# Weight pieces of 512 columns instead of 256 for v and for the last gate of a hybrid decoder layer, and v as a whole ahead of the recurrent branch

## The chip, the cores and the metric

The kernel runs on one core of one Trainium2 chip. What counts is the time of an execution on the device, in microseconds (us); the figure for a kernel is the median of its runs. A profile is of one execution, whose own time stands beside it.

## What is computed

One decoder layer in fp32 on 512 positions of width 1024, and a last RMSNorm:

```python
h = rmsnorm(x, norm_mix_g)
u_x, u_g, q, k, v, g_lru, g_att = split(h @ w_in)           # w_in: 1024 x 7168
c = causal_depthwise_conv(u_x, conv_w, conv_b)
y_lru = rg_lru(c, w_rgate, b_rgate, w_igate, b_igate, lam) * gelu(u_g)
y_att = stick_breaking_attention(q, k, v)                    # 16 heads of 64
merged = sigmoid(g_lru) * (y_lru @ w_br_lru) + sigmoid(g_att) * (y_att @ w_br_att)
x = x + merged @ w_out
x = x + square(relu(rmsnorm(x) @ w_mlp_up)) @ w_mlp_down     # 4096 wide
x = x + sigmoid(rmsnorm(x) @ w_ple_gate) * (p @ w_ple)
out = rmsnorm(x, norm_final_g)
```

The multipliers of a norm are folded: a product is made with x times the gain, and the reciprocal root of a row is multiplied in afterwards, where the rows lie on partitions.

## The kernel before

**Products.** Every fp32 product is made of three matmuls. `split` (L51 to L53) cuts a tile into a rounded part `hi` (a cast on ScalarE, L52) and the rest `lo` (a subtraction on VectorE, L53); `prod` (L115 to L121) then adds hi·hi (L119), hi·lo (L120) and lo·hi (L121) in one accumulator. For most products the weights are the stationary operand and 512 positions of the activations stream by (`proj`, L125). v and the last gate are the other way round, since their rows (positions) must lie on partitions: 128 positions of the activations are stationary and the weight columns stream by, 256 at a time. Such a product is named by its block of positions `tb` (0 to 3) and its piece of columns.

**Weights.** `load_raw` (L46) fetches 512 KB into one of three buffers `raw`, `split` writes it to `whi` and `wlo`, also three buffers each. `next_half` (L103) hands out the piece that is ready and starts on the next of the list `halves`; so loads run two or three pieces ahead of the matmuls, and a cast waits until the matmuls are done with the buffer that it overwrites.

**Order.** Engines work off their instructions in order. The order in the program is set by a scheduler that places instructions by modelled times; the code sets dependences, buffers and a few priorities.

**v before** (L214 to L273, L382 to L386). x arrives in eight row tiles of 128 x 512, and with each the rows of the first weight piece. `xg` is x times the gain, split. v is made in four pieces of 256 columns: `v0` row tile by row tile as x comes in, `v1` and `v2` behind it, all with xg; `v_evac` multiplies them by `rcol`, the reciprocal roots, on the way out. Meanwhile the sums of squares are made, turned into `rcol`, spread over all partitions by matmuls (`bc_x`, L186), and `hT`, the normed x, is made from them (L262, then L52 and L53). All later projections take hT. `v3` follows only behind the recurrent branch, with hT. Accumulators: a pool `pst` of four banks for v0 and v2, `pp` of three banks for v1 and for all that `proj` makes up to the attention, so that the first product of the recurrent branch, `ps_ux`, takes a bank of `pp`.

**Recurrent branch** (L276 to L380). Eight products `ps_ux`, each followed by a convolution on VectorE and the small gate products `pg`; then eight products `ps_ug`. The second half of the recurrence, `lru_mid(1)`, is a chain of 128 x 2048 instructions on ScalarE and VectorE, with four scans (L347) and the multiplication L379 at its end. Attention tiles (`qs`, `kh`) lie where the branch's tiles lay, so their first writer waits for L379.

**Last gate** (L589 to L654). For four pieces of 256 columns and four blocks of positions, `gate_rows` makes a product `pgt`; `gate_post` applies the sigmoid (L609), multiplies by `ple` and adds to x (L610, L611), sums squares (L612) and multiplies by the last gain (L614). `last_norm` scales and stores a block.

Of the kernel before, what the change touches and what calls it, by code (L numbers as in the profile page):

```python
# [31 lines left out]
def hybrid_layer(ctx, tc, xT, pT, vecs, gfin, gates, w_in, w_bl, w_ba, w_out,  # L32
# [185 lines left out]
    def v_evac(ch, tb, ps, scale):  # L218
        hi = vs[:, 2 * ch:2 * ch + 2, tb, 0:4:3, :]
        lo = vs[:, 2 * ch:2 * ch + 2, tb, 1:3, :]  # L220
        src = ps.rearrange("p (a b d) -> p a b d", a=2, b=2)
        if scale is None:
            split(hi, lo, src)
        else:
            sc.activation(hi, src, AF.Copy, scale=scale)
            for a in range(2):
                ve.scalar_tensor_tensor(lo[:, a], src[:, a], scale, f32(hi[:, a]),
                                        op0=ALU.mult, op1=ALU.subtract)

    def v_pairs(act, w, tb):  # L230
# [368 lines left out]
    def gate_rows(tb, q):  # L599
        t = slice(tb * P, (tb + 1) * P)  # L600
        ps = pq.tile([P, 256], F32, tag="pp", name=f"pgt{tb}_{q}")
        prod(ps, [(h3[:, 0, k, t], h3[:, 1, k, t], wq[q][k // 4][0][:, k % 4, :],
                   wq[q][k // 4][1][:, k % 4, :]) for k in range(KT)])
        return ps

    def gate_post(tb, q, ps):
        c = slice(q * 256, (q + 1) * 256)
        sg = sgs[(q + tb) % 4]
# [25 lines left out]
    wq.append([next_half("pg1_0")])  # L634
    behind = ctx.enter_context(ExitStack())
    behind.enter_context(tc.issue_after(scaled.ins))
    for i, (hi, lo) in ((3, (wb3[:, 0], wb3[:, 1])), *((4 + j, (wb1[:, 2 * j], wb1[:, 2 * j + 1]))
                                                       for j in range(4))):
        split(hi, lo, load_raw(w_pg[i // 2][:, (i % 2) * 1024:(i % 2 + 1) * 1024], f"pg{i}"))
        if i % 2 == 0:  # L640
            wq.append([])
        wq[i // 2].append(tuple(t.rearrange("p (k n) -> p k n", k=4) for t in (hi, lo)))
# [84 lines left out]
```

## Time and profile before

| | us |
|---|---|
| median of three runs | 945.73 |
| the three runs | 943.81, 945.73, 948.19 |
| the profiled execution, its own time | 946.11 |
| its span, from the first instruction to the last | 944.0 |
| TensorE busy in the span | 929.5 |
| VectorE busy | 542.4 |
| ScalarE busy | 471.3 |

The profile page gives busy times, a chain of work that ended last, and groups of instructions; the trace answers for single lines, tiles and stretches of time. TensorE's time is listed as PE, its weight loads as PEld, VectorE as DVE, ScalarE as ACT. A matmul's duration in the listing is from its start to its modelled end and overlaps the next one's; the pace is the distance from start to start.

### The profile page before, as it was taken

To read this page: it belongs to the slowest core of one execution; us is meant where nothing else is said; L and a number is where in the kernel's file an instruction comes from. 1 tells how busy PE (TensorE), PEld (TensorE's weight loads), DVE (VectorE), ACT (ScalarE), POOL (GpSimd) and SP (SyncE) were. 2 spreads that over 40 slices of the span, in tenths; PEclk is the share of its full clock that TensorE was granted. 3 is DMA by queue.
4 is the path that set the end of the run, shared out by engine and by line. 5 is a ranking of instruction groups with operands and counts; after the bars stand their busy time and mean duration, and the time that the engine had idled before them with its cause. 6 is when DMAs were issued, how large, how long until landed. Compare 5 with 4: busy or idle time off the path is not lost.

```text
span 944.0 us, 12123 instructions
## 1 busy us (share of the span) xinstructions
PE 929.5 (98%) x4634; PEld 790.9 (84%) x4634; DVE 542.4 (57%) x818; ACT 471.3 (50%) x751; POOL 67.9 (7%) x147
## 2 busy tenths in 40 slices
PE   8999999999999999999999999999999999999996
PEld 7988888888888888888888888888888888888896
DVE  6796947688998986534655433333333333344476
ACT  6567676667776765412334444541214554333443
POOL 0010000133233332000000000000000000000000
PEclk9999999999999999999999999999999999999998
DMA  6241222211222222432232223323223223222312
GB/s 220 95 134 67 90 90 85 95 68 67 68 68 68 67 68 68 173 111 95 90 109 92 90 90 104 119 90 101 100 90 108 94 89 107 94 90 90 112 45 90
DMA packets 25401, 89.42 MB, mean 95 GB/s; under 512 B 2944, under 2 KB 3200, under 8 KB 25088
## 3 DMA queue, kind: packets, MB, share of 16 engines
q1 hardware_dynamic: 24768, 87.61, 27.5%
q10 hardware_dynamic: 576, 1.05, 0.3%
q8 instruction: 36, 0.59, 0.3%
q14 instruction: 21, 0.17, 0.1%
HBM read 86.55 MB, written 2.10 MB: 94 GB/s over the span
## 4 chain that ended last, share of the span: by engine, by line
PE 95%; ACT 2%; DVE 1%; DMA 1%; issue 1%; SPq 0%; ACTq 0%
PE ps_up L119 6%; PE dn L121 6%; PE ps_up L121 6%; PE dn L119 6%; PE dn L120 6%; PE ps_up L120 6%; PE t L445 2%; PE pgt L120 2%; PE pgt L121 2%; PE pgt L119 2%; PE ps_gl L121 2%; PE ps_k L121 2%; PE ps_q L119 2%; PE ps_ga L121 2%; PE ps_q L120 2%; PE ps_k L119 2%
## 5 line engine op out<-in xcount | busy, mean ns | idle before, releaser
L119 PE MATMUL dn<-ah,whi_dn 128*128 128x512 f32 x256 | 100.2, 391 | 0.0
L119 PE MATMUL ps_up<-h,whi_up 128*128 128x512 f32 x256 | 99.9, 390 | 0.0
L121 PE MATMUL ps_up<-h,wlo_up 128*128 128x512 f32 x256 | 99.7, 390 | 0.0
L121 PE MATMUL dn<-ah,wlo_dn 128*128 128x512 f32 x256 | 99.7, 389 | 0.0
L120 PE MATMUL ps_up<-h,whi_up 128*128 128x512 f32 x256 | 99.6, 389 | 0.0
L120 PE MATMUL dn<-al,whi_dn 128*128 128x512 f32 x256 | 99.6, 389 | 0.0
L52 ACT CAST whi_dn<-raw_dn 128x1024 fp32r<-128x1024 f32 x32 | 33.6, 1053 | 108.3 <-PE dn L120 82.9
L53 DVE TENSOR_TENSOR wlo_up<-raw_up,whi_up 128x1024 fp32r<-128x1024 f32 x32 | 39.2, 1224 | 73.4 <-ACT whi_up L52 73.4
L52 ACT CAST whi_up<-raw_up 128x1024 fp32r<-128x1024 f32 x32 | 33.7, 1054 | 91.3 <-PE ps_up L120 62.9
L53 DVE TENSOR_TENSOR wlo_dn<-raw_dn,whi_dn 128x1024 fp32r<-128x1024 f32 x32 | 39.0, 1222 | 67.6 <-ACT whi_dn L52 67.6
L432 DVE TENSOR_TENSOR_SCAN pr<-r,zero 128x128 f32<-128x128 f32 (+1 forms) x64 | 54.1, 845 | 10.7 <-POOL r L155 10.2
L121 PEld LDWEIGHTS dn<-ah,wlo_dn 128*128 128x128 f32 x256 | 48.1, 188 | 10.1
L121 PEld LDWEIGHTS ps_up<-h,wlo_up 128*128 128x128 f32 x256 | 48.1, 188 | 10.0
L120 PEld LDWEIGHTS ps_up<-h,whi_up 128*128 128x128 f32 x256 | 48.1, 188 | 10.0
L120 PEld LDWEIGHTS dn<-al,whi_dn 128*128 128x128 f32 x256 | 48.1, 188 | 9.8
L119 PEld LDWEIGHTS ps_up<-h,whi_up 128*128 128x128 f32 x256 | 48.1, 188 | 9.8
L119 PEld LDWEIGHTS dn<-ah,whi_dn 128*128 128x128 f32 x256 | 48.1, 188 | 9.7
L155 POOL TENSOR_SCALAR_AFFINE_SELECT r<-r 128x128 f32<-128x128 f32 x64 | 29.8, 466 | 192.6 <-ACT r L428 190.2
L428 ACT ACTIVATE r<-z 128x128 f32<-128x128 f32 (+1 forms) x64 | 28.5, 445 | 27.7 <-PE z L424 27.0
L580 DVE TENSOR_TENSOR d<-dn,sumsq 128x512 f32<-128x512 f32 x16 | 11.1, 692 | 52.1 <-PE dn L121 52.1
L155 POOL TENSOR_SCALAR_AFFINE_SELECT s<-s 128x128 f32<-128x128 f32 x64 | 33.6, 525 | 5.1 <-ACT s L430 3.3
L434 DVE TENSOR_TENSOR s<-s,pr 128x127 f32<-128x127 f32 (+1 forms) x64 | 31.8, 498 | 3.6
(282 smaller groups left out, 2424.0 us busy)
## 6 DMA issues: line engine op xcount, KB each, us to landing
raw_up<-in_w_up_dram SPq DMA_DIRECT2D x32, 512.0 KB, 3.4
raw_dn<-in_w_dn_dram SPq DMA_DIRECT2D x32, 512.0 KB, 3.5
raw_u<-in_w_in_dram SPq DMA_DIRECT2D x16, 512.0 KB, 3.6
raw_qk<-in_w_in_dram SPq DMA_DIRECT2D x16, 512.0 KB, 3.5
raw_gl<-in_w_in_dram SPq DMA_DIRECT2D x8, 512.0 KB, 3.4
raw_ga<-in_w_in_dram SPq DMA_DIRECT2D x8, 512.0 KB, 3.4
raw_bl<-in_w_bl_dram SPq DMA_DIRECT2D x8, 512.0 KB, 3.4
raw_ba<-in_w_ba_dram SPq DMA_DIRECT2D x8, 512.0 KB, 3.4
```

The lines of the kernel that those rows point to most:

```text
L52: sc.copy(hi, src)
L53: ve.tensor_tensor(lo, src, f32(hi), op=ALU.subtract)
L119: pe.matmul(ps, lh, rh, start=(first and i == 0), stop=False)
L120: pe.matmul(ps, lh, rl, start=False, stop=False)
L121: pe.matmul(ps, ll, rh, start=False, stop=(last and i == n - 1))
L155: gp.affine_select(block, block, pattern=[[-1, P]], compare_op=ALU.is_gt, fill=fill, base=0, channel_multiplier=1)
L428: sc.activation(r[:, 0:w], z[:, 0:w], AF.Sigmoid, scale=-0.125)
L432: ve.tensor_tensor_scan(pr[:, 0:w][:, ::-1], r[:, 0:w][:, ::-1], zero.broadcast_to([P, w]), 1.0, op0=ALU.mult, op1=ALU.add)
L434: ve.tensor_tensor(s[:, 0:w - 1], s[:, 0:w - 1], pr[:, 1:w], op=ALU.mult)
L445: turned[kbs[0]] = pe.transpose(pt[:, o:o + P], att[qb][:, kb * P:(kb + 1) * P], ident)
L580: ve.tensor_tensor(t, ps, rs2, op=ALU.mult)
```

## The change

v is made in two pieces of 512 columns, both ahead of the recurrent branch and both with xg. Its weights come in chunks of two row tiles by 512 columns (512 KB as before), eight chunks `v0_0` to `v1_3`. Of the first piece, six row tiles are loaded beside x, in three chunks, and the fourth chunk through `next_half`. The second piece runs chunk by chunk, over the four blocks of positions in each; three of its accumulators are in `pp`, the fourth in `pst`. `v_evac` takes 512 columns: one ScalarE instruction and four on VectorE. The stage `v3` behind the recurrent branch is gone.

The gate has two pieces of 512 columns. For the first, all four blocks run over row tiles 0 to 5, and then over 6 and 7; the second piece of the last block is still made as two of 256. `gate_post` takes 512 columns; the sum of a block's squares has two terms instead of four (three for the last block). The weights are laid out accordingly on the host. The core of the diff:

```diff
-    for i in range(3):
-        order(f"v{i}", w_in[i], 4)
+    for i in range(2):
+        for j in range(4):
+            halves.append((f"v{i}_{j}", w_in[2 * i + j // 2][:, (j % 2) * 1024:(j % 2 + 1) * 1024], 2))
     for i in range(8):
         order(f"u{i}", w_in[4 + i], 8)
-    order("v3", w_in[3], 4)
...
-    for a, b in ((0, 1), (1, 2), (2, 4), (4, 6), (6, 8)):
+    for a, b in ((0, 1), (1, 2), (2, 4), (4, 6)):
+        if a != 1:
+            raw0.append(wp.tile([P, 1024], F32, tag="raw", name=f"raw_v0_{a // 2}"))
         sy.dma_start(x32[:, a:b, :], xT[:, a:b, :])
-        sy.dma_start(raw0[a // 4][:, a % 4:(b - 1) % 4 + 1, :], src0[:, a:b, :])
+        c = slice((a % 2) * 512, ((b - 1) % 2 + 1) * 512)
+        sy.dma_start(raw0[-1][:, c], halves[a // 2][1][:, c])
+    sy.dma_start(x32[:, 6:8, :], xT[:, 6:8, :])
...
-        ps0 = [pst.tile([P, 256], F32, tag="pv", name=f"pv0_{tb}") for tb in range(NB)]
+        ps0 = [pst.tile([P, S], F32, tag="pv", name=f"pv0_{tb}") for tb in range(NB)]
         for k in range(KT):
+            if k == 6:
+                w.append(next_half("v0_3"))
             for tb in range(NB):
-                prod(ps0[tb], v_pairs(xg, w, tb)[k:k + 1], first=(k == 0), last=(k == KT - 1))
+                prod(ps0[tb], v_pairs(xg, w, [k], tb), first=(k == 0), last=(k == KT - 1))
...
-        w = next_pair("v1")
-        psv = [pp.tile([P, 2, 256], F32, tag="pp", name=f"pv1_{i}") for i in range(2)]
-        for tb in range(NB):
-            prod(psv[tb // 2][:, tb % 2, :], v_pairs(xg, w, tb))
...
+        ps1 = [(pp if tb < 3 else pst).tile([P, S], F32, tag="pp" if tb < 3 else "pv", name=f"pv1_{tb}")
+               for tb in range(NB)]
         for tb in range(NB):
             v_evac(0, tb, ps0[tb], rcol[:, tb:tb + 1])
+        for j in range(4):
+            w = [None] * j + [next_half(f"v1_{j}")]
+            for tb in range(NB):
+                prod(ps1[tb], v_pairs(xg, w, [2 * j, 2 * j + 1], tb), first=(j == 0), last=(j == 3))
         for tb in range(NB):
-            v_evac(1, tb, psv[tb // 2][:, tb % 2, :], rcol[:, tb:tb + 1])
-        w = next_pair("v2")
-        for tb in range(NB):
-            ps = pst.tile([P, 256], F32, tag="pv", name=f"pv2_{tb}")
-            prod(ps, v_pairs(xg, w, tb))
-            v_evac(2, tb, ps, rcol[:, tb:tb + 1])
+            v_evac(1, tb, ps1[tb], rcol[:, tb:tb + 1])
...
-        w = next_pair("v3")
-        for tb in range(NB):
-            ps = pp.tile([P, 256], F32, tag="pp", name=f"pv3_{tb}")
-            prod(ps, v_pairs(hT, w, tb))
-            v_evac(3, tb, ps, None)
...
-    wq = [next_pair("pg0")]
-    first = [gate_rows(tb, 0) for tb in range(3)]
+    wq = [[next_half(f"pg0_{j}") for j in range(3)], []]
+    rows = [pq.tile([P, S], F32, tag="pp", name=f"pgt{tb}_0") for tb in range(NB)]
+    for tb in range(NB):
+        gate_rows(rows[tb], tb, range(0, 6))
...
     for tb in range(NB):
-        gate_post(tb, 2, gate_rows(tb, 2))
+        gate_rows(rows[tb], tb, range(6, 8))
+        gate_post(tb, 0, 512, rows[tb])
+    for tb in range(NB):
+        w = 512 if tb < NB - 1 else 256
...
+        for a in range(512, 1024, w):
+            ps = pq.tile([P, w], F32, tag="pp", name=f"pgt{tb}_{a}")
+            gate_rows(ps, tb, range(0, KT), slice(a - 512, a - 512 + w), 1)
```

VectorE before, between the spreading of the norm and the first product of the recurrent branch; `bc_x` is the spread norm, `vs` the evacuated v, `pv2_0` its third piece for the first block:

```order
L262 SCALAR_TENSOR_TENSOR x32_68<-x32_68,vt_67,bc_x_409 128x512 x7
L227 SCALAR_TENSOR_TENSOR vs_105<-pv1_1_293,rcol_279,vs_105 128x128 [waits Activation_49]
L227 SCALAR_TENSOR_TENSOR vs_105<-pv1_1_293,rcol_279,vs_105 128x128
L53 TENSOR_TENSOR hT_106<-x32_68,hT_106 128x512 [waits Activation_49]
L227 SCALAR_TENSOR_TENSOR vs_105<-pv2_0_482,rcol_279,vs_105 128x128 [waits Activation_49]
L227 SCALAR_TENSOR_TENSOR vs_105<-pv2_0_482,rcol_279,vs_105 128x128
L53 TENSOR_TENSOR hT_106<-x32_68,hT_106 128x512 [waits Activation_49] x2
L227 SCALAR_TENSOR_TENSOR vs_105<-pv2_1_510,rcol_279,vs_105 128x128 [waits Activation_49]
L227 SCALAR_TENSOR_TENSOR vs_105<-pv2_1_510,rcol_279,vs_105 128x128
L53 TENSOR_TENSOR hT_106<-x32_68,hT_106 128x512 [waits Activation_49] x4
```

The same place of the changed kernel; `pv1_0` is the second piece of 512 columns for the first block:

```order
L265 SCALAR_TENSOR_TENSOR x32_68<-x32_68,vt_67,bc_x_303 128x512 [waits PE_49]
L265 SCALAR_TENSOR_TENSOR x32_68<-x32_68,vt_67,bc_x_303 128x512 x7
L53 TENSOR_TENSOR wlo_u0_0_457<-raw_u0_0_454,whi_u0_0_456 128x1024 [waits DMAHW7_49,Activation_49]
L53 TENSOR_TENSOR hT_106<-x32_68,hT_106 128x512 [waits Activation_49] x7
L53 TENSOR_TENSOR wlo_u0_1_562<-raw_u0_1_559,whi_u0_1_561 128x1024 [waits DMAHW1_49,Activation_49]
L53 TENSOR_TENSOR hT_106<-x32_68,hT_106 128x512 [waits Activation_49]
L227 SCALAR_TENSOR_TENSOR vs_105<-pv1_0_340,rcol_283,vs_105 128x128 [waits Activation_49]
L227 SCALAR_TENSOR_TENSOR vs_105<-pv1_0_340,rcol_283,vs_105 128x128 x3
```

The evacuations of v's last pieces stood between the parts of hT before, and stand behind all of them now.

TensorE in the changed kernel, at the end of v and the beginning of the recurrent branch; `dg_x3` belongs to the last part of the spreading:

```order
L188 MATMUL bc_x_303<-dg_x3_313,onesf_87 128x128 [waits DVE_49]
L121 MATMUL pv1_3_343<-whi_v1_1_366,xg_113 128x512
L119 MATMUL pv1_0_340<-whi_v1_2_396,xg_113 128x512 [waits Activation_49]
...
L119 MATMUL pv1_0_340<-whi_v1_3_426,xg_113 128x512 [waits Activation_49]
...
L121 MATMUL pv1_3_343<-whi_v1_3_426,xg_113 128x512
L119 MATMUL ps_ux0_558<-hT_106,whi_u0_0_456 128x512 [waits DVE_49,Activation_49]
```

Between the spreading and `ps_ux0` 49 matmuls of v are left, and `ps_ux0` waits for VectorE with its first matmul.

VectorE before, at the end of the recurrent branch; L347 are the scans, L379 the multiplication that ends the branch, `qs0` and `kl` the first tiles of the attention:

```order
L347 SCALAR_TENSOR_TENSOR i1_877<-a1_1347,r1_876 128x512 x3
L53 TENSOR_TENSOR vs_105<-pv3_0_1381,vs_105 128x2x128 [waits Activation_49]
L53 TENSOR_TENSOR vs_105<-pv3_1_1408,vs_105 128x2x128 [waits Activation_49]
L379 TENSOR_TENSOR y_lru_1075<-i1_877,y_lru_1075 128x2048 [waits DVE_49]
L53 TENSOR_TENSOR vs_105<-pv3_2_1435,vs_105 128x2x128 [waits Activation_49]
L53 TENSOR_TENSOR wlo_qk0_1_1518<-raw_qk0_1_1515,whi_qk0_1_1517 128x1024 [waits DMAHW3_49,Activation_49]
L53 TENSOR_TENSOR vs_105<-pv3_3_1462,vs_105 128x2x128 [waits Activation_49]
```

The same place of the changed kernel (the scans are L351, the multiplication L383):

```order
L349 TENSOR_TENSOR r1_786<-r1_786,i1_787 128x2048 [waits Activation_49]
L53 TENSOR_TENSOR wlo_qk1_0_1339<-raw_qk1_0_1336,whi_qk1_0_1338 128x1024 [waits DMAHW2_49,PE_49,Activation_49]
L351 SCALAR_TENSOR_TENSOR i1_787<-a1_1257,r1_786 128x512 [waits DVE_49]
L351 SCALAR_TENSOR_TENSOR i1_787<-a1_1257,r1_786 128x512 x3
L53 TENSOR_TENSOR wlo_qk1_1_1531<-raw_qk1_1_1528,whi_qk1_1_1530 128x1024 [waits DMAHW3_49,PE_49,Activation_49]
L383 TENSOR_TENSOR y_lru_985<-i1_787,y_lru_985 128x2048 [waits DVE_49]
L53 TENSOR_TENSOR wlo_gl0_0_1562<-raw_gl0_0_1559,whi_gl0_0_1561 128x1024 [waits DMAHW4_49,PE_49,Activation_49]
L408 TENSOR_TENSOR qs0_1366<-ps_q0_1304,qs0_1366 64x512 [waits Activation_49]
L411 TENSOR_TENSOR kl_1301<-ps_k0_1335,kh0_1367 64x512 [waits Activation_49]
```

The four evacuations of v3 are gone, and the weights of q and k of the second pair (`qk1`) stand ahead of the scans and of the multiplication. On TensorE three projections (q0, k0, q1, 72 matmuls) follow the last `ps_ug` directly, then the first scores, which read `qs0`, `kh0` and `kl`; before, v3's 96 matmuls came first, and the scores stood behind q0, k0, q1 and four matmuls of k1.

## Rows read from the trace of the kernel before

**Rows 1.** Page: busy time of each engine, its share of the span, instructions.

```profile
PE 929.5 (98%) x4634; PEld 790.9 (84%) x4634; DVE 542.4 (57%) x818; ACT 471.3 (50%) x751; POOL 67.9 (7%) x147
```

**Rows 2.** Waits of TensorE: total us, times, longest us.

```profile
PE pv L119 <- ACT whi_v L52: 2.9, 2, 2.5
...
PE pv L119 <- DVE vs L53: 1.6, 1, 1.6
```

**Rows 3.** Matmul groups of 256 columns (line, shapes, count | busy us, mean ns | idle).

```profile
L119 PE MATMUL pv<-whi_v,xg 128*128 128x256 f32 x96 | 24.3, 301 | 2.9 <-ACT whi_v L52 2.9
L119 PE MATMUL pgt<-wb,h 128*128 128x256 f32 x80 | 22.6, 283 | 0.0
...
L119 PE MATMUL pgt<-whi_pg,h 128*128 128x256 f32 x48 | 13.7, 286 | 0.0
...
L119 PE MATMUL pv<-whi_v,hT 128*128 128x256 f32 x32 | 9.0, 286 | 1.6 <-DVE vs L53 1.6
```

**Rows 4.** Timeline (start us, us, what), TensorE, in the MLP's second half.

```profile
880.41 0.39 PE L121 MATMUL dn<-ah,wlo_dn 128*128 128x512 f32 x1
...
887.21 0.39 PE L121 MATMUL dn<-ah,wlo_dn 128*128 128x512 f32 x1
```

**Rows 5.** Timeline, ScalarE, last gate: the last weight cast, sigmoids of 256 columns.

```profile
904.46 1.05 ACT L52 CAST wb<-raw_pg 128x1024 fp32r<-128x1024 f32 x1 [0.73 <-DMA raw_pg<-in_w_pg_dram]
...
912.42 0.47 ACT L609 ACTIVATE work<-pgt,rs 128x256 f32<-128x256 f32 x1 [0.33 <-PE pgt L121]
...
921.06 0.47 ACT L609 ACTIVATE work<-pgt,rs 128x256 f32<-128x256 f32 x1 [0.89 <-PE pgt L121]
```

**Rows 6.** Timeline, TensorE, the beginning.

```profile
5.84 1.22 PE L119 MATMUL pv<-whi_v,xg 128*128 128x256 f32 x4 [0.43 <-ACT whi_v L52]
...
9.18 0.28 PE L121 MATMUL pv<-whi_v,xg 128*128 128x256 f32 x1
11.94 0.74 PE L119 MATMUL pv<-whi_v,xg 128*128 128x256 f32 x4 [2.48 <-ACT whi_v L52]
```

**Rows 7.** Timeline, ScalarE, the third and fourth row tile of x.

```profile
9.73 1.33 ACT L56 ACTIVATE xg<-x,vt 128x512 fp32r<-128x512 f32 x2 [2.14 <-DMA x<-in_xT_dram]
```

**Rows 8.** Stretches: busy us (count) of PE, PEld, DVE, ACT, POOL; PEclk; DMA; GB/s.

```profile
6.00:8.00 2.00, 2.00 (x14) 2.00 (x15) 1.80 (x4) 1.34 (x3) 0.00 (x0) 1.00 0.76 200
...
12.00:14.00 2.00, 1.78 (x12) 1.58 (x13) 2.00 (x5) 2.00 (x5) 0.00 (x0) 0.94 0.90 363
14.00:16.00 2.00, 2.00 (x12) 2.00 (x11) 2.00 (x5) 2.00 (x5) 0.00 (x0) 0.50 0.79 277
16.00:18.00 2.00, 2.00 (x14) 2.00 (x14) 2.00 (x4) 2.00 (x5) 0.00 (x0) 0.70 0.03 12
```

**Rows 9.** Timeline, VectorE, ahead of the recurrent branch.

```profile
36.51 1.12 DVE L227 SCALAR_TENSOR_TENSOR vs<-pv,rcol,vs 128x128 fp32r<-128x128 f32 x4
...
38.67 5.35 DVE L262 SCALAR_TENSOR_TENSOR x<-x,vt,bc_x 128x512 f32<-128x512 f32 x8
...
47.31 2.48 DVE L53 TENSOR_TENSOR hT<-x,hT 128x512 fp32r<-128x512 f32 x4
...
50.83 1.21 DVE L53 TENSOR_TENSOR wlo_u<-raw_u,whi_u 128x1024 fp32r<-128x1024 f32 x1
```

**Rows 10.** Timeline, TensorE, from the last `ps_ug` through v3.

```profile
145.92 0.39 PE L121 MATMUL ps_ug<-hT,wlo_u 128*128 128x512 f32 x1
...
154.66 0.28 PE L121 MATMUL pv<-whi_v,hT 128*128 128x256 f32 x1
156.50 0.39 PE L119 MATMUL pv<-whi_v,hT 128*128 128x256 f32 x1 [1.56 <-DVE vs L53]
```

**Rows 11.** Timeline, VectorE, from the branch's end to the first kl.

```profile
156.69 2.28 DVE L379 TENSOR_TENSOR y_lru<-i,y_lru 128x2048 f32<-128x2048 f32 x1
...
172.75 0.68 DVE L414 TENSOR_TENSOR kl<-ps_k,kh 64x512 fp32r<-64x512 f32 x1
```

**Rows 12.** Timeline, ScalarE, ahead of the first qs.

```profile
164.92 1.05 ACT L52 CAST whi_qk<-raw_qk 128x1024 fp32r<-128x1024 f32 x1 [3.92 <-PE ps_q L120]
```

More of the change, by code (lines that the diff above doesn't have):

```diff
@@ L99, in hybrid_layer @@
             order(f"dn{h}_{i}", w_dn[8 * h + i], 8)
-    order("pg0", w_pg[0], 4)
-    halves.append(("pg1_0", w_pg[1][:, 0:1024], 4))
+    for j in range(3):
+        halves.append((f"pg0_{j}", w_pg[0][:, j * 1024:(j + 1) * 1024], 2))
     state = {"i": 0, "ready": None}
@@ L218, in v_evac, with v_pairs @@
     def v_evac(ch, tb, ps, scale):
[L219 to L230, printed above, removed]
+        hi = vs[:, 4 * ch:4 * ch + 4, tb, 0:4:3, :]
+        lo = vs[:, 4 * ch:4 * ch + 4, tb, 1:3, :]
+        src = ps.rearrange("p (a b d) -> p a b d", a=4, b=2)
+        sc.activation(hi, src, AF.Copy, scale=scale)
+        for a in range(4):
+            ve.scalar_tensor_tensor(lo[:, a], src[:, a], scale, f32(hi[:, a]),
+                                    op0=ALU.mult, op1=ALU.subtract)
+    def v_pairs(act, w, ks, tb):
         t = slice(tb * P, (tb + 1) * P)
-        return [(act[:, 0, k, t], act[:, 1, k, t], w[k // 4][0][:, k % 4, :], w[k // 4][1][:, k % 4, :])
-                for k in range(KT)]
+        return [(act[:, 0, k, t], act[:, 1, k, t], w[k // 2][0][:, k % 2, :], w[k // 2][1][:, k % 2, :])
+                for k in ks]
     with tc.tile_pool(name="st", bufs=1) as st, \
@@ L589, in hybrid_layer @@
     work = big2.tile([P, 8192], F32, tag="B3", name="work")
-    gf, junk = work[:, 0:1024], work[:, 1024:1280]
+    gf, junk = work[:, 0:1024], work[:, 1024:1536]
     outs = [work[:, 2048 + i * 1024:3072 + i * 1024] for i in range(4)]
-    sgs = [work[:, 6144 + i * 256:6400 + i * 256] for i in range(4)]
+    sgs = [work[:, 6144 + i * 512:6656 + i * 512] for i in range(2)]
     sy.dma_start(gf, gfin.broadcast_to([P, D]))
@@ L597, in hybrid_layer, with gate_rows, gate_post @@
     ssc = const.tile([P, 4 * NB], F32, name="ssc")
-    def gate_rows(tb, q):
+    def gate_rows(ps, tb, ks, c=slice(0, 512), h=0):
         t = slice(tb * P, (tb + 1) * P)
[L601 to L608, printed above, removed]
+        prod(ps, [(h3[:, 0, k, t], h3[:, 1, k, t], wq[h][k // 2][0][:, k % 2, c],
+                   wq[h][k // 2][1][:, k % 2, c]) for k in ks], first=(ks[0] == 0), last=(ks[-1] == KT - 1))
+    def gate_post(tb, a, n, ps):
+        c = slice(a, a + n)
+        sg = sgs[tb % 2][:, 0:n]
         sc.activation(sg, ps, AF.Sigmoid, scale=rs3[:, tb:tb + 1])
@@ L633, in hybrid_layer @@
     wb3 = big.tile([P, 2, 1024], F32R, tag="F1", name="wb3")
-    wq.append([next_half("pg1_0")])
     behind = ctx.enter_context(ExitStack())
@@ L638, in hybrid_layer @@
                                                        for j in range(4))):
[L639 to L642, printed above, removed]
+        split(hi, lo, load_raw(w_pg[i // 4][:, (i % 4) * 1024:(i % 4 + 1) * 1024], f"pg{i}"))
+        wq[i // 4].append(tuple(t.rearrange("p (k n) -> p k n", k=2) for t in (hi, lo)))
     behind.close()
-    for q in range(2):
-        for tb in range(NB):
-            gate_post(tb, q, first[tb] if q == 0 and tb < 3 else gate_rows(tb, q))
     for tb in range(NB):
-        gate_post(tb, 2, gate_rows(tb, 2))
+        gate_rows(rows[tb], tb, range(6, 8))
+        gate_post(tb, 0, 512, rows[tb])
+    for tb in range(NB):
+        w = 512 if tb < NB - 1 else 256
         s012 = fin.tile([P, 1], F32, tag="ss", name=f"ssf{tb}")
-        ve.tensor_reduce(s012, ssc[:, 4 * tb:4 * tb + 3], axis=mybir.AxisListType.X, op=ALU.add)
-        ve.tensor_scalar(s012, s012, 1.0 / D, EPS, op0=ALU.mult, op1=ALU.add)
-        gate_post(tb, 3, gate_rows(tb, 3))
+        for a in range(512, 1024, w):
+            ps = pq.tile([P, w], F32, tag="pp", name=f"pgt{tb}_{a}")
+            gate_rows(ps, tb, range(0, KT), slice(a - 512, a - 512 + w), 1)
+            if a + w == 1024:
+                head = ssc[:, 4 * tb + 1:4 * tb + 2]
+                if w == 256:
+                    ve.tensor_tensor(s012, head, ssc[:, 4 * tb + 2:4 * tb + 3], op=ALU.add)
+                    head = s012
+                ve.tensor_scalar(s012, head, 1.0 / D, EPS, op0=ALU.mult, op1=ALU.add)
+            gate_post(tb, a, w, ps)
         last_norm(tb, s012)
@@ L686, in _layout @@
     wi = wi.reshape(56, P, KT, P)[order].reshape(28, 2, P, KT, P)
-    wi = np.concatenate([wi[:4].transpose(0, 2, 3, 1, 4).reshape(4, P, 2048),
+    wv = wi[:4].reshape(2, 4, P, KT, P).transpose(0, 2, 3, 1, 4).reshape(2, P, 2, 2048)
+    wi = np.concatenate([wv.transpose(0, 2, 1, 3).reshape(4, P, 2048),
                          wi[4:].transpose(0, 2, 1, 3, 4).reshape(24, P, 2048)])
```

29 lines of the change are left out of this document (16 added, 13 removed).

## The prediction

> **What bounds the kernel now.** I read the busy times first: TensorE works 929.5 of 944.0 us, 98% of the span, VectorE 57%, ScalarE 50% [rows 1]. So the change is worth what it does to the pace of TensorE's matmuls and to TensorE's few waits. The list of those waits comes second. Two belong to v: 2.5 us at the start, where the third row tile of x and its weights aren't there yet, and 1.6 us at v3 [rows 2]. Third, the groups of 256 columns: the three lines of a product count alike, so v has 3 × (96 + 32) = 384 such matmuls and the gate 3 × (80 + 48) = 384, and the gate's never waited [rows 3]. Last, the pace, from start to start in undisturbed stretches: 30 matmuls of 512 columns in 887.21 − 880.41 = 6.80 us, 0.2267 us each [rows 4]; three blocks of 24 matmuls of 256 columns between two sigmoids, 921.06 − 912.42 = 8.64 us for 72, 0.1200 us each [rows 5].
>
> **Matmuls: −4.8 us.** All 384 of v and 336 of the gate become 512 wide (the last block's second piece, 48, stays): 360 pairs. A pair takes 2 × 0.1200 = 0.2400 us, one of 512 columns 0.2267: 13.3 ns less, 360 times, 4.8 us (2.6 in v, 2.2 in the gate). TensorE has no cover, so it counts in full. No row shows a matmul of 512 columns with positions stationary. From below the saving is nothing (time by the column); from above it is the 13.3 ns, since the three matmuls of a product in rows 4 have the same form of 128 x 512. I take 13.3, the row of equal shape.
>
> Here a rule speaks against the change. The Trainium skill, "TensorE: Matmul & The Clock Gate", section "Back-to-back issue gap", gives the gap of lone warm matmuls as columns over 2.4 GHz plus 2.5 ns, so that a pair would save only 2.5 ns; 360 pairs would save 0.9 us by it, an estimate. The rows here disagree: they show 120.0 and 226.7 ns, where it has 109 and 216.
>
> **Start: −1.1 us.** Before, TensorE runs two row tiles from 5.84 to 9.30 and sits idle until 11.94, 2.48 us of it listed as waiting for ScalarE's cast [rows 6], which was held by x arriving for 9.73 and by ScalarE's two scaled copies of 1.33 us [rows 7]. The 24 matmuls took 3.46 us instead of 24 × 0.12 = 2.88: 0.6 us of slow beginning. After, each row tile brings 256 KB of weights instead of 128. The first cast is twice as long, +0.2 us (an estimate, counted below); then 24 × 0.2267 + 0.6 = 6.0 us of work, until 12.1. The x tiles three and four arrive behind 0.26 MB more: at the 363 GB/s of the stretch 12 to 14 [rows 8] 0.7 us, so ScalarE begins at 10.4 and TensorE 2.2 us after that as before, plus 0.8 (two wider casts at 0.2, and 0.13 MB more ahead of the third tile's weights, 0.4), at 13.5: a wait of 1.4 us instead of 2.5. Best is 0.6, without the 0.8. With 200 GB/s, the rate of 6 to 8 [rows 8], the 0.52 MB more up to the fourth tile's weights are 2.6 us, TensorE goes on at some 14.7 and the wait is 2.6. I take 1.4, since both tiles are fetched in the busier stretch. Behind that wait stands all of v, as before. Later row tiles have 12 × 0.2267 = 2.7 us of work each, for 512 KB that at 363 GB/s take 1.4: no wait.
>
> **First matmul later: +0.2 us**, the wider cast.
>
> **v3's wait goes: −1.7 us.** TensorE's last matmul before it began at 154.66, the next at 156.50 [rows 10]; less 0.12 that is 1.7. With the stage gone nothing waits there. What is next late is the attention's start, below.
>
> **New wait at `ps_ux0`: +2.4 us.** The second piece's accumulator `pv1_0` has the bank of `pp` that `ps_ux0` takes, so its first matmul waits until VectorE has evacuated `pv1_0`, and in the order that stands behind all of the normed x. From the spreading on, VectorE needs 5.35 for the eight multiplications, 1.21 for weights, 8 × 0.62 for hT, 1.21 for weights and 1.12 for four subtractions [rows 9]: 13.85 us, some 13.4 with the overlaps that the rows show (eight of 0.69 in 5.35). TensorE has 49 × 0.2267 = 11.1 us of v left. The wait is 2.3 to 2.75; I take 2.4. Before, the pieces were evacuated between parts of hT and TensorE ran through. Behind the waiting matmul on TensorE is the whole recurrent branch; ScalarE's copies and VectorE's convolution wait for that, with no work of their own that would hide it. The three other evacuations, 3.4 us, come while `ps_ux0` runs (24 × 0.2267 = 5.4 us) and cost nothing. Scaled evacuations are as many as before, and those of v3 fall away.
>
> **Clock: 0.** After the idle stretch before 11.94 the granted clock fell from 1.00 to 0.50 and then read 0.70 [rows 8], its two levels being 2.4 and 1.2 GHz: 0.06 × 2 + 0.50 × 2 + 0.30 × 2 = 1.7 us of work lost. The wait of 1.6 at v3 isn't the length that was followed by this; 2.48 was. So I expect no fall behind the start's 1.4 (−1.7) and one behind the 2.4 at `ps_ux0` (+1.7). Bounds: −1.7 if neither, +1.7 if both.
>
> **Branch to attention: 0.** Count from T, the end of the last `ps_ug`, 145.92 + 0.23 = 146.15 [rows 10]. v3 covered this place with 96 matmuls. Now TensorE is ready for the first scores after 72 matmuls of q0, k0 and q1, at T + 16.3, and they need `qs0` and `kl`, whose tiles are free only when L379 has ended. That was at 156.69 + 2.28 = 158.97, T + 12.8 [rows 11]. In the new order one weight subtraction of 1.21 replaces 0.73 of v3's ahead of it: T + 13.3. Then come weights 1.21, `qs0` 0.68 and `kl` 0.68: T + 15.9, 0.4 ahead of need. From above: the first `kl` ended at 172.75 + 0.68, T + 27.3 [rows 11], which would be a wait of 11.0. But ScalarE stood 3.92 us for q0's matmuls there [rows 12], which v3 had put back, so I take 0.
>
> **Last gate: 0.** The weights of its second piece are needed after 96 × 0.2267 = 21.8 us instead of 192 × 0.12 = 23.0, and are asked for some 1.4 us later, since the norm's sums, which release them, stand behind 35 matmuls of 512 columns where 54 of 256 stood (7.9 against 6.5 us). The last were cast from 904.46 on [rows 5], for 1.05, and subtracted in 1.21: done at 906.7, now at 908.1. The sigmoid of 912.42 [rows 5] is that of the eighth block, with which the first half of the gate's columns ends, so the need was at about 912.1 and is now at 910.8; for the last weights it is 18 matmuls, 4.1 us, later. Cost 0, at worst the 2.6 by which need and request draw together. The work behind the last matmul is as before.
>
> **Sum.** −4.8 − 1.1 + 0.2 − 1.7 + 2.4 + 0 = −5.0. From the profiled execution's own 946.11 (span 944.0) that is 941.1; it lies 0.4 above the median of 945.73, from which the forecast is 940.7.
>
> **Rivals.**
> - *The clock stays up behind `ps_ux0`.* TensorE's wait there is near the v3 one, which was no cause of a fall; −1.7: 939.0. Against it: 2.4 is nearer to 2.48 than to 1.6.
> - *The start gains nothing.* At 200 GB/s the wait is 2.6 (+1.2) and the clock falls there too (+1.7): 943.6. For it: the first row tiles came at that rate. Against: later ones didn't.
> - *The change doesn't do what it says*, time goes by the column: +4.8, 945.5. The Trainium skill's gap, cited above, would give 944.6, an estimate. For it: no row of this kind; against it: the two paces of rows 4 and 5, both steady.
> - *Slower: the scores wait for the recurrent branch.* If `qs0` and `kl` come late because ScalarE's and VectorE's weight work stands ahead of L379 and of `kl`, TensorE waits up to 11.0 us at T + 16.3: 951.7. From 5.0 us of wait on the kernel is slower than before, from 9.7 on by over 0.5%. For it: the margin is 0.4 us and v3's 13.3 us of cover are gone. Against: of the 27.3 us most was waiting for TensorE itself.
>
> **How the numbers follow.** Chances: forecast 0.46 (940.7, its own range 939.7 to 942.0 from the bounds at the start and at `ps_ux0`), clock up 0.20, start without gain 0.18, columns 0.07, scores 0.09. The range goes from 937.8 (clock up, and the start's best) to 944.9, which leaves out the upper half of the columns' case and most of the scores'. A measurement of this kernel tells some 0.5% from no change, 4.7 us: faster means below 941.0. That takes somewhat over half of the forecast's 0.46 and the 0.20 of the clock: 0.45. Slower is above 950.5, half of the scores' 0.09 and a rest: 0.06. The remaining 0.49 is the same.
>
> **What would show it.** In the changed kernel's groups v and gate read 128x512, and 24 of them in a row take 5.44 us (5.76 if time goes by the column). TensorE's waits list about 1.4 us at the start, none for v's last stage, and one of `ps_ux0` for VectorE's `vs` of about 2.4; the granted clock is 1.00 in the stretches after the start and falls for some 3 us after `ps_ux0` begins. The first scores wait for no `kl` and no `qs`. Wrong would be a wait of several us at the first scores, or at the gate's second piece for its weights, or a start that waits longer than 2.5.

## The result and the profile after

| | before | after |
|---|---|---|
| median, us | 945.73 | 941.22 |
| the runs, us | 943.81 to 948.19 (7) | 940.31 to 942.0 (7) |
| the profiled execution, its own time | 946.11 | 941.22 |
| its span | 944.0 | 939.5 |

The ratio of after to before is 0.9948, with a 95% interval from 0.9934 to 0.9962: 4.5 us less, where the forecast was 940.7, 5.0 less.

The page of the changed kernel, busy times, which answer [rows 1]:

```profile
PE 925.9 (99%) x4274; PEld 772.0 (82%) x4274; DVE 542.5 (58%) x795; ACT 466.5 (50%) x719; POOL 67.4 (7%) x147
```

TensorE is busy 3.6 us less and has 360 matmuls fewer. Its waits (total us, times, longest us), which answer [rows 2]:

```profile
PE ps_ux L119 <- DVE vs L227: 2.5, 1, 2.5
PE wt L164 <- POOL onesf L151: 1.2, 1, 1.2
PE pv L119 <- ACT whi_v L52: 0.8, 1, 0.8
```

v3's wait and that of the third row tile are gone; the new one at `ps_ux0` is 2.5 long. The 0.8 stands ahead of the first matmul of v. The groups (line, shapes, count | busy us, mean ns | idle), which answer [rows 3]:

```profile
L120 PE MATMUL pv<-wlo_v,xg 128*128 128x512 f32 x64 | 25.6, 400 | 0.1
...
L120 PE MATMUL pgt<-wb,h 128*128 128x512 f32 x32 | 12.4, 389 | 0.0
L120 PE MATMUL pgt<-wlo_pg,h 128*128 128x512 f32 x24 | 9.4, 390 | 0.0
```

The beginning on TensorE (start us, us, what), which answers [rows 6]:

```profile
6.20 2.07 PE L119 MATMUL pv<-whi_v,xg 128*128 128x512 f32 x4 [0.79 <-ACT whi_v L52]
8.07 0.63 PE L120 MATMUL pv<-wlo_v,xg 128*128 128x512 f32 x1
8.50 0.63 PE L121 MATMUL pv<-whi_v,xg 128*128 128x512 f32 x1
...
10.62 1.07 PE L119 MATMUL pv<-whi_v,xg 128*128 128x512 f32 x4
...
13.34 1.11 PE L119 MATMUL pv<-whi_v,xg 128*128 128x512 f32 x4
```

The first row tile takes 10.62 − 6.20 = 4.42 us, the second 13.34 − 10.62 = 2.72, which is 12 × 0.2267. The third begins without a wait and takes 16.48 − 13.34 = 3.14. From `ps_ux0` to the first scores and in the gate, on TensorE, which answers [rows 10]:

```profile
56.43 0.47 PE L119 MATMUL ps_ux<-hT,whi_u 128*128 128x512 f32 x1 [2.54 <-DVE vs L227]
...
156.47 0.39 PE L121 MATMUL ps_ug<-hT,wlo_u 128*128 128x512 f32 x1
156.69 0.39 PE L119 MATMUL ps_q<-hT,whi_qk 128*128 128x512 f32 x1
...
173.01 0.39 PE L420 MATMUL z<-kh,qs 128*128 128x128 f32 x2
173.24 0.39 PE L421 MATMUL z<-kl,qs 128*128 128x128 f32 x2
...
885.00 0.48 PE L119 MATMUL pgt<-whi_pg,h 128*128 128x512 f32 x1
...
930.27 0.28 PE L121 MATMUL pgt<-wb,h 128*128 128x256 f32 x1
```

In the kernel before the same places stand at 47.44 (`ps_ux0`), 145.92 (last `ps_ug`), 159.48 (first q0), 887.79 and 935.14 (first and last of the gate). From these starts the 4.5 us of the two spans can be booked, beside the forecast's terms. v's matmuls are booked at the paces of the prediction, which both traces of the changed kernel show again in v (12 matmuls in 2.72 us). "Start" is what is left of `ps_ux0`'s start without v's matmuls and without its own wait: 47.44 − 288 × 0.1200 = 12.88 before, 56.43 − 2.54 − 192 × 0.2267 = 10.36 after.

| us | forecast | the two traces |
|---|---|---|
| v's matmuls (192 × 13.3 ns) | −2.6 | −2.6 |
| start, with its clock | −1.1 + 0.2 − 1.7 | −2.5 |
| wait at `ps_ux0` | +2.4 | +2.5 |
| clock behind `ps_ux0` | +1.7 | +1.6 (100.04 to the last `ps_ug`, 98.48 before) |
| v3's wait | −1.7 | −1.8 (13.56 from the last `ps_ug` to q0, now 0.22; less 96 × 0.12) |
| q0 to the gate | 0 | 0 (728.31 both) |
| gate | −2.2 | −2.1 (47.35, now 45.27) |
| behind the last matmul | 0 | +0.4 (8.9, now 9.2) |
| sum | −5.0 | −4.5, as the spans |

### The profile page after: what moved, and what is told of

Read it like the earlier page. It is cut to its first block, busy times and chain, and to the rows that moved or that the text cites. A ratio compares the mean times of both kernels' runs of the same rounds, so it can differ in the third digit from the quotient of the medians.

```text
span 939.5 us, 11336 instructions
## 1 busy us (share of the span) xinstructions
PE 925.9 (99%) x4274; PEld 772.0 (82%) x4274; DVE 542.5 (58%) x795; ACT 466.5 (50%) x719; POOL 67.4 (7%) x147
```

## The experiments

**The change once more.** The same kernel, in the rounds of the next three.

> The changed kernel once more, on the chip and in the rounds in which its parts are timed. By the result so far: 4.5 us less than before (ratio 0.995). Its profile, from another execution, tells which of the stretches are steady: the matmul pace of v, 0.2267 us, the wait of about 2.5 us at ps_ux0 with a lower clock behind it, and no wait at the attention's start should stand again; where in the first 10 us the clock rises may differ.

941.45 us, ratio 0.9953 (0.9940 to 0.9967). The profiled execution, of 939.84, shows the wait of 2.55 at `ps_ux0` and no lower clock behind it. Stretches of this execution (TensorE's busy time and count stand first behind the length, the granted clock stands third from the end):

```profile
54.00:56.00 2.00, 0.06 (x1) 0.00 (x0) 2.00 (x5) 1.62 (x2) 1.82 (x2) 1.00 0.15 27
56.00:58.00 2.00, 1.40 (x6) 1.21 (x7) 2.00 (x9) 1.95 (x2) 1.81 (x3) 1.00 0.60 240
58.00:60.00 2.00, 2.00 (x11) 1.62 (x10) 2.00 (x10) 1.43 (x2) 0.00 (x0) 1.00 0.00 0
60.00:62.00 2.00, 2.00 (x11) 1.65 (x10) 1.97 (x3) 0.00 (x0) 0.00 (x0) 1.00 0.11 18
```

The same in the first trace of the changed kernel:

```profile
54.00:56.00 2.00, 0.00 (x0) 0.00 (x0) 2.00 (x6) 1.70 (x3) 1.99 (x2) 1.00 0.24 55
56.00:58.00 2.00, 1.57 (x6) 1.31 (x7) 2.00 (x9) 1.96 (x3) 1.64 (x3) 0.85 0.54 211
58.00:60.00 2.00, 2.00 (x6) 1.55 (x5) 2.00 (x9) 1.27 (x1) 0.00 (x0) 0.50 0.00 0
60.00:62.00 2.00, 2.00 (x9) 1.63 (x8) 1.97 (x3) 0.00 (x0) 0.00 (x0) 0.80 0.12 31
```

Six matmuls in the stretch from 58 to 60 instead of eleven. After the same idle stretch the clock fell to its lower level in one execution and stayed in the other. Of the 13 timed executions of this kernel, four have a mean granted clock of 0.997 and times of 939.5 to 940.8, nine have 0.995 or 0.996 and 941.0 to 942.3. Only two of the 13 were traced, and a mean doesn't tell where the clock fell, so the sorting of the others is a reading.

**The two halves of the change, each alone.**

v alone (the gate's parts of the diff left out):

```diff
-    for i in range(3):
-        order(f"v{i}", w_in[i], 4)
+    for i in range(2):
+        for j in range(4):
+            halves.append((f"v{i}_{j}", w_in[2 * i + j // 2][:, (j % 2) * 1024:(j % 2 + 1) * 1024], 2))
...
-        w = next_pair("v3")
...
     order("pg0", w_pg[0], 4)
```

> The kernel before with the change of v alone; the gate stays at 256 columns. The prediction's terms for v sum to -2.8 us: pace -2.6, start -1.1 and +0.2, v3's wait -1.7, ps_ux0's wait +2.4, clock 0. So 942.9 where the kernel before takes 945.7, a ratio of 0.997. The rival, time by the column, has no -2.6: 945.5. If the gate is what brings the whole gain, v_only is at 945.7 or above. In the profile the q0 of the attention should begin some 2.8 us earlier than in the kernel before, and the last matmul come 8.9 us before the span's end, as there.

942.97 us, ratio 0.9970 (0.9959 to 0.9981), against 945.67 of the kernel before in the same rounds: −2.7, forecast −2.8. In its trace q0 begins at 156.54, 2.9 us earlier than before.

The gate alone (v's parts left out):

```diff
     order("v3", w_in[3], 4)
...
-    order("pg0", w_pg[0], 4)
-    halves.append(("pg1_0", w_pg[1][:, 0:1024], 4))
+    for j in range(3):
+        halves.append((f"pg0_{j}", w_pg[0][:, j * 1024:(j + 1) * 1024], 2))
```

> The kernel before with the change of the gate alone; v stays at 256 columns and in its places. By the pace, 168 pairs at 13.3 ns are 2.2 us up to the last matmul; the changed kernel showed 2.1 there and 0.4 us more behind the last matmul, so 1.7 to 2.2 us less than before: 943.5 to 944.0, ratio 0.998. Time by the column: 945.7 to 946.1. From the gate's first matmul to its last, about 45.2 us, where the kernel before has 47.4.

944.12 us, ratio 0.9985 (0.9976 to 0.9994): −1.55, and 933.06 − 887.79 = 45.27 us from the gate's first matmul to its last, as in the whole change; 1.7 to 2.2 had been expected of the time. The halves sum to 4.25 of the whole's 4.2 to 4.5: no help or hindrance between them is seen.

This kernel has v as before, and its trace shows something of the start. TensorE there:

```profile
10.30 0.75 PE L119 MATMUL pv<-whi_v,xg 128*128 128x256 f32 x4 [2.65 <-ACT whi_v L52]
13.44 0.74 PE L119 MATMUL pv<-whi_v,xg 128*128 128x256 f32 x4 [1.45 <-ACT whi_v L52]
...
47.45 0.40 PE L119 MATMUL ps_ux<-hT,whi_u 128*128 128x512 f32 x1
```

Here the clock didn't fall, and TensorE waited 4.7 us for v's weights in all, where the trace of before has 2.9 and a fall [rows 2, 8]. `ps_ux0` begins at 47.45 in the one and 47.44 in the other. That doesn't make the fall free, for in this execution the third and fourth row tile of x came 1.5 us later, as ScalarE's copies show (9.73 before [rows 7]):

```profile
11.24 1.33 ACT L56 ACTIVATE xg<-x,vt 128x512 fp32r<-128x512 f32 x2 [0.99 <-DMA x<-in_xT_dram]
```

So the third row tile began at 13.44 instead of 11.94, and from there to `ps_ux0` it took 34.01 us instead of 35.50. Late loads in the one and the low clock in the other came to the same, by chance; by these two traces the fall cost the kernel before 1.5 us on top of its wait. ScalarE, too, was 1.5 us ahead there and stayed so (it cast the next piece at 18.82, here at 20.33), which speaks against TensorE having had to wait in that time anyway.

**Pairs of 256 columns in the new order.** Each matmul of 512 columns in v and the gate cut into two:

```diff
+    def halved(ps, pairs, first, last):
+        for a in range(0, ps.shape[-1], 256):
+            c = slice(a, a + 256)
+            prod(ps[:, c], [(lh, ll, rh[:, c], rl[:, c]) for lh, ll, rh, rl in pairs],
+                 first and a == 0, last and a + 256 == ps.shape[-1])
...
-                prod(ps0[tb], v_pairs(xg, w, [k], tb), first=(k == 0), last=(k == KT - 1))
+                halved(ps0[tb], v_pairs(xg, w, [k], tb), first=(k == 0), last=(k == KT - 1))
```

> The changed kernel with each matmul of 512 columns in v and in the gate cut into two of 256, one half behind the other in the same accumulator; loads, pieces, buffers and stages stay as changed. It measures the pace by itself. By the pace the gate takes 2.2 us longer and v 2.6. In its order the second half of the spreading stands ahead of 143 matmuls of 256 columns of v, 17.2 us, where VectorE needs 13.4, so the wait at ps_ux0 (2.5 us) and the clock's fall behind it (1.7) should be gone: in all 4.8 - 4.2 = 0.6 us slower than the changed kernel, about 941.8. If time goes by the column, the 4.2 alone are left: 937.0. If the wait stays, 946.

941.57 us, ratio 0.9959 (0.9947 to 0.9970): 0.1 to 0.4 above the changed kernel, where 0.6 was expected, and far from 937.0. TensorE in its trace:

```profile
55.93 0.28 PE L127 MATMUL pv<-whi_v,xg 128*128 128x256 f32 x1
56.05 0.40 PE L125 MATMUL ps_ux<-hT,whi_u 128*128 128x512 f32 x1
...
882.96 0.36 PE L125 MATMUL pgt<-whi_pg,h 128*128 128x256 f32 x1
...
930.31 0.28 PE L127 MATMUL pgt<-wb,h 128*128 128x256 f32 x1
```

The gate takes 47.35 us again, 2.08 more than with 512 columns: 12.4 ns for each of the 168 pairs. `ps_ux0` follows v's last matmul after 0.12 without a wait. So the pace is worth nearly what the forecast says, and the wait depends on how much of v stands behind the spreading. The Trainium skill's section "Back-to-back issue gap" ("TensorE: Matmul & The Clock Gate"), by whose gap of lone matmuls a pair would save 2.5 ns, an estimate, does not agree with this trace.

**`ps_ux0` with a free bank.**

```diff
-        ps1 = [(pp if tb < 3 else pst).tile([P, S], F32, tag="pp" if tb < 3 else "pv", name=f"pv1_{tb}")
+        ps1 = [(pp if tb < 2 else pst).tile([P, S], F32, tag="pp" if tb < 2 else "pv", name=f"pv1_{tb}")
```

> The changed kernel with v's second piece in two accumulators of pp and two of pst, instead of three and one, so that ps_ux0 takes a bank of pp that is free. Theory: the wait of 2.5 us at ps_ux0 comes from that bank alone and stood on the path, so ps_ux0 begins at about 53.9 instead of 56.4 and the kernel is 2.5 us faster in executions in which the clock stayed up, 4.1 us where it fell behind the wait: median about 937.5, ratio to the kernel before 0.991. Rival: hT isn't ready much earlier either, or ps_ux1 waits in its place, then less than 1 us is gained: 940.5 or more.

937.26 us, ratio 0.9909 (0.9896 to 0.9923). TensorE in its trace, at `ps_ux0` and at the first scores:

```profile
53.43 0.39 PE L119 MATMUL ps_ux<-hT,whi_u 128*128 128x512 f32 x1
...
169.24 0.47 PE L119 MATMUL ps_k<-hT,whi_qk 128*128 128x512 f32 x1 [0.25 <-DVE qs L408]
```

No wait at `ps_ux0`, and mean granted clocks of 0.997 and 0.998 in all its runs. One line of the program takes 4.0 to 4.2 us off the changed kernel's two medians, which are from other rounds; the intervals lie apart. In the trace 0.5 comes back later: from q0 to the gate it takes 880.84 − 152.05 = 728.79 us instead of 728.31, with a wait for `qs`, and the recurrent branch ends 13.75 us behind the beginning of q0 instead of 13.31. It isn't the free bank's price as such: the kernels with single loads, below, have the same bank and take 728.30 to 728.33. What puts the branch's end off here stays open.

**The wait filled with work.** Eleven needless matmuls ahead of `ps_ux0`:

```diff
+        fill = pst.tile([P, S], F32, tag="ps", name="fill", bufs=1)
+        for i in range(11):
+            pe.matmul(fill, hT[:, 1, 4, 0:P], hT[:, 0, 0, :], start=(i == 0), stop=(i == 10))
```

> The changed kernel with eleven needless matmuls of 512 columns (2.5 us) ahead of ps_ux0, into an accumulator that nothing reads, so that TensorE works through the wait. It parts the wait's own price from the clock's. If the lower clock behind ps_ux0 follows from the idle stretch, it is gone in every execution: no time of 941 and above, all between 939.5 and 940.8, a median of 940. If the clock falls whether TensorE idles or not, the times spread as in the changed kernel, 939.5 to 942.3.

940.29 us, ratio 0.9942 (0.9929 to 0.9954), all five times between 939.54 and 940.79. Stretches of its trace, where `ps_ux0` begins at 57.02:

```profile
56.00:58.00 2.00, 1.95 (x9) 1.33 (x8) 2.00 (x9) 1.67 (x3) 2.00 (x2) 1.00 0.70 262
58.00:60.00 2.00, 2.00 (x10) 1.64 (x9) 2.00 (x11) 0.56 (x1) 0.24 (x3) 1.00 0.00 0
60.00:62.00 2.00, 2.00 (x11) 1.65 (x10) 2.00 (x4) 0.00 (x0) 0.00 (x0) 1.00 0.00 0
```

The wait's own price is paid, the clock's isn't: five executions without a time in the upper group, where nine of 13 had one. The traces of all runs agree. Five have the idle stretch of 2.5 us at `ps_ux0`, and from there to the last `ps_ug` four of them take 100.04 to 100.10 us (the changed kernel, v alone, and the two runs that follow) and one takes 98.48 (the changed kernel once more); the nine without it take 98.37 to 98.51. So the clock's fall follows the idle stretch, though not every time. The mean clock is a weaker sign: this trace reads 0.996 without a fall there, since in every trace the clock is low behind the last matmul too.

**More to load at the start.** Two row tiles of x loaded twice, 512 KB ahead of the third tile:

```diff
+        if a == 2:
+            sy.dma_start(x32[:, 6:8, :], xT[:, 6:8, :])
         sy.dma_start(x32[:, a:b, :], xT[:, a:b, :])
```

> The changed kernel with 512 KB more loaded at the start: the last two row tiles of x come a first time ahead of the third and fourth, and again in their place. If the loads set the pace of the first 15 us, the third tile's weights come 0.52 MB later, at the 400 to 420 GB/s that the changed kernel's trace shows there 1.3 us, and ps_ux0 begins at 57.7 instead of 56.4; the time is 942.6. If TensorE's own work and its clock set it, ps_ux0 stays at 56.4 and the time at 941.3.

942.93 us, ratio 0.9972 (0.9962 to 0.9982). TensorE, the second and third row tile and `ps_ux0`, and behind it ScalarE's copies of the third and fourth tile of x:

```profile
11.09 1.07 PE L119 MATMUL pv<-whi_v,xg 128*128 128x512 f32 x4
15.03 1.20 PE L119 MATMUL pv<-whi_v,xg 128*128 128x512 f32 x4 [1.06 <-ACT whi_v L52]
...
58.22 0.47 PE L119 MATMUL ps_ux<-hT,whi_u 128*128 128x512 f32 x1 [2.54 <-DVE vs L229]
...
12.09 1.34 ACT L56 ACTIVATE xg<-x,vt 128x512 fp32r<-128x512 f32 x2 [1.92 <-DMA x<-in_xT_dram]
```

`ps_ux0` is 1.6 to 1.8 us later than in the two traces of the changed kernel, though the beginning ran at the lower clock in the first of them and here. The third row tile begins 2.94 us behind the beginning of ScalarE's copies (15.03 and 12.09), as in the changed kernel once more (13.43 and 10.49). So x's arrival sets when the third row tile can begin. In the first trace of the changed kernel, 13.34 and 10.31, TensorE was itself busy until then: there both limits nearly meet.

**The margin at the attention.** One more instruction on VectorE at the end of the recurrent branch:

```diff
                 ve.tensor_tensor(yg, hs, yg, op=ALU.mult)
+                if g == 1:
+                    ve.tensor_scalar(yg, yg, 1.0, None, op0=ALU.mult)
```

> The changed kernel with one needless multiplication by 1 of 128 x 2048 on VectorE behind the one that ends the recurrent branch, ahead of qs0 and kl: some 1.8 us. In the changed kernel the first kl ended 0.7 us before the scores that read it. If that margin is all there is since v3's matmuls no longer stand there, TensorE now waits about 1.2 us at the first scores and the time is 942.5. If there is more slack, it waits for nothing and the time stays at 941.3.

942.56 us, ratio 0.9966 (0.9954 to 0.9978). TensorE at the first scores:

```profile
172.97 0.39 PE L121 MATMUL ps_q<-hT,wlo_qk 128*128 128x512 f32 x1
173.44 0.47 PE L422 MATMUL z<-kh,qs 128*128 128x128 f32 x2
174.07 0.49 PE L423 MATMUL z<-kl,qs 128*128 128x128 f32 x2 [0.16 <-DVE kl L413]
174.88 0.47 PE L119 MATMUL ps_k<-hT,whi_qk 128*128 128x512 f32 x1 [0.32 <-DVE qs L410]
```

From q0 to the gate 886.49 − 156.88 = 729.61 us, 1.3 more than without. But the added instruction took less than the 1.8 us expected:

```profile
170.22 1.23 DVE L385 TENSOR_SCALAR y_lru<-y_lru 128x2048 f32<-128x2048 f32 x1
```

So all of the delay is paid, and the agreement of the time with the expected 942.5 is luck: the slack wasn't the 0.7 us at the first `kl`. In the changed kernel it was smaller one step further on. Behind the first scores TensorE begins k1, which waits for `qs` here and in the kernel with the free bank; there VectorE's second `qs`, from q0's accumulator, ended 0.2 us before k1 began:

```profile
172.59 0.69 DVE L408 TENSOR_TENSOR qs<-ps_q,qs 64x512 fp32r<-64x512 f32 x1
...
173.47 0.43 PE L119 MATMUL ps_k<-hT,whi_qk 128*128 128x512 f32 x1
```

That v3's matmuls would have hidden such a delay follows from the order; no run shows it.

**Single loads for the third and fourth row tile**, on top of the free bank:

```diff
-    for a, b in ((0, 1), (1, 2), (2, 4), (4, 6)):
-        if a != 1:
+    for a, b in ((0, 1), (1, 2), (2, 3), (3, 4), (4, 6)):
+        if a % 2 == 0:
```

> The kernel with v's accumulators two and two, and besides the third and fourth row tile of x and their weights loaded one by one (x, weights, x, weights, 256 KB each) instead of in two loads of 512 KB. If the loads set the pace of the first 15 us, the third tile's weights arrive 0.52 MB earlier and TensorE no longer waits at the third tile, 0.6 us for the cast and some 0.5 for the rest of it in the trace of the kernel with two and two: ps_ux0 begins at 52.4 instead of 53.4 and the time is 936.2 instead of 937.3. If TensorE's own pace sets it, nothing changes: 937.3.

> The kernel with v's accumulators two and two once more, in the rounds of the one with split loads: 937.3 again, ratio to the kernel before 0.991, and ps_ux0 without a wait in another execution.

935.67 us, ratio 0.9896 (0.9881 to 0.9911), against 937.35 and 0.9911 (0.9895 to 0.9928) for the free bank alone in the same rounds: −1.7, where 1.1 was expected. The intervals overlap. In the traces `ps_ux0` begins at 53.41 with single loads, where 52.4 was expected, and at 53.43 and 54.78 without; the first of these ran its beginning at the lower clock, the other two didn't. With single loads TensorE waits for no weights of v but the first, so there its own pace set the start. Some 0.4 us of the difference lies at the attention, where the wait for `qs` is gone. What the loads alone are worth is not shown.

**No idle stretch ahead of v**, on top of that: twelve instead of nine of the matmuls that stand ahead of it.

```diff
-        for i in range(9):
+        for i in range(12):
             pe.matmul(wt, onesf, onesf, start=True, stop=True)
```

> The kernel with split loads and v's accumulators two and two, and twelve instead of nine matmuls ahead of v that only keep TensorE busy, so that it no longer stands idle from 5.4 to 6.1. In the trace of the kernel with split loads the first ten matmuls of v ran at the lower clock, to 9.7, and two of its four times, 934.8 and 934.9, lie 1.6 to 1.9 below the other two. If the idle stretch ahead of v keeps the clock low in some executions, all times now lie at 935. If the moment at which the clock rises doesn't depend on it, they spread as before, 934.8 to 936.7, or lie 0.2 higher for the longer start.

> The kernel with split loads once more, in the rounds of the one with twelve matmuls ahead of v: 935.7 and a spread from 934.8 to 936.7, the upper times with a mean granted clock of 0.996 and the lower with 0.997.

935.33 us, ratio 0.9885 (0.9871 to 0.9900), four times from 934.71 to 935.61, against 935.88, ratio 0.9888 (0.9870 to 0.9906), with 934.75, 935.29, 936.47 and 936.89 for nine. TensorE with twelve:

```profile
6.83 1.37 PE L119 MATMUL pv<-whi_v,xg 128*128 128x512 f32 x4
8.04 0.39 PE L120 MATMUL pv<-wlo_v,xg 128*128 128x512 f32 x1
...
9.88 1.07 PE L119 MATMUL pv<-whi_v,xg 128*128 128x512 f32 x4
```

The first row tile takes 3.05 us here, 4.8 with nine (6.31 to 11.15). Four executions without an upper time, beside four of eight with nine matmuls: this agrees with the idle stretch keeping the clock low, but four are too few to settle it. This kernel has the lowest median of the study, 10.6 us below the kernel before in its rounds; against nine matmuls the intervals overlap.

## Why the prediction was right, step by step

**Matmuls, −4.8: right.** v's pace is the forecast's, and the gate is 2.08 us shorter; cutting the matmuls again gave these 2.08 back. Where the 0.15 lies that the gate lacks stays open.

**Start, −1.1 and +0.2, and clock there, −1.7: right, each within 0.4.** The forecast had the third row tile begin at 13.5; it began at 13.34, in the second trace at 13.43. Less the matmuls of two row tiles (24 × 0.1200 before, 24 × 0.2267 now) that is −1.2 and −1.1, where −0.9 was forecast. From there to `ps_ux0`, less v's matmuls and the wait there, TensorE spends 2.46 and 2.53 us where it spent 3.82: −1.3 to −1.4 for a fall of the clock that no longer happens, where −1.7 was forecast. The kernel with the gate alone, which has v as before, spends 2.33 without a fall, so the fall's price was 1.5; the third row tile gave some of it back, with 3.14 us instead of 2.72. What the forecast had wrong is how the time up to 13.4 passes. It counted 0.6 us of slow beginning and a wait of 1.4. In the first trace the beginning ran at the lower clock and lost 4.42 − 2.72 = 1.7 us, and there was no wait at all; in the second it lost 0.3, with waits of 0.76 and 0.52. Since x's arrival allows the third row tile no earlier in either, the sum was nearly the same; that the slow beginning of 1.7 still fitted ahead of it was luck.

**v3's wait, −1.7: right**, −1.8.

**New wait at `ps_ux0`, +2.4: right**, 2.54, for the reason given: with another bank it was gone, and nothing else waited in its place but, in that kernel's two traces, 0.5 us at the attention. VectorE's part began 0.65 us behind the beginning of the last part of the spreading and ran as counted.

**Clock behind `ps_ux0`, +1.7: right in size, not in certainty.** It is 1.6 where it happens and happens in part of the executions; the rival of 939.0 is therefore no rival but the same kernel in other executions (939.5 to 940.8). That the median came out near the forecast is luck to this extent: it lies in the larger group. The two traces with v3's 1.6 us of idle time show no fall behind it, but two are few where the fall is a matter of chance, and no run here varied the length of the wait. In the rounds of the experiments four executions of the kernel before have a mean clock of 0.993 and take 947.3 to 947.7 us, where 43 others have 0.995 to 0.998 and take 944.2 to 947.1; none of the four was traced, so a fall behind v3's wait in some of them isn't excluded.

**Attention, 0: right, and tighter than foreseen.** VectorE in the changed kernel, which answers [rows 11]:

```profile
167.71 2.29 DVE L383 TENSOR_TENSOR y_lru<-i,y_lru 128x2048 f32<-128x2048 f32 x1
169.91 1.22 DVE L53 TENSOR_TENSOR wlo_gl<-raw_gl,whi_gl 128x1024 fp32r<-128x1024 f32 x1
171.16 0.68 DVE L408 TENSOR_TENSOR qs<-ps_q,qs 64x512 fp32r<-64x512 f32 x1
171.88 0.68 DVE L411 TENSOR_TENSOR kl<-ps_k,kh 64x512 fp32r<-64x512 f32 x1
```

Counted from 156.69, the multiplication ends at 13.3 and `kl` at 15.9, as forecast, and the scores begin at 16.3. The place that the forecast left out is k1, whose first matmul comes only 0.2 us behind the second `qs`. The slower rival was real as a mechanism: 1.23 us more on VectorE cost 1.3.

**Last gate's weights, 0: right**; no wait is listed there. **Behind the last matmul, 0: off by 0.4**: VectorE's last scaling begins 4.60 us behind the last matmul instead of 4.45, as the block before it is now one piece of 512 and finishes later; the rest is in the last store.

**The other rivals.** A start without gain at 200 GB/s: the trace has 217 from 6 to 8 but 401 to 422 from 8 to 14, so the rate of the first stretch wasn't the one that counted. Time by the column: ruled out by the cut matmuls.

**The range.** Its lower end of 937.8 is lower than its terms give: with the clock up 939.0, less 0.8 for the start's best, 938.2. Nothing hangs on it.

## What to carry to other kernels

Where an accumulator's bank passes to the next product, the evacuation's place in VectorE's queue is what the product waits for; count the queue up to it, and see whether another bank is free, since one index was worth about as much here as the whole change. Two executions can come to the same point at the same time for different reasons, late loads in one and a low clock in the other: compare the stretches in between, and when the loads came, before calling a cost hidden. And a stage that is moved away takes its cover with it: count the chain that it hid up to everything that waits for it, the next product in an accumulator's bank as well as the first reader, to a tenth of a microsecond if the margin is that small.

## What was not expected of the hardware

The same idle stretch of 2.5 us was followed by the lower clock in one trace of the changed kernel and not in the other, at a price of 1.6 us (100.04 and 98.48), and the timed executions seem to fall into two groups accordingly. And the granted clock of the first microseconds can't be read from the stretches: this one reads 1.00 in the changed kernel,

```profile
6.00:8.00 2.00, 1.80 (x4) 1.49 (x5) 1.82 (x3) 1.30 (x3) 0.00 (x0) 1.00 0.69 217
```

while its matmuls of 512 columns begin 0.43 us apart (8.07, 8.50), which is 512 columns at 1.2 GHz. The pace, and not the column, shows the level there.
